# A hybrid decoder block on one Trainium2 core: due times for a plan's last weight splits, a sum of weights by an adding transfer, and the norm's ScalarE steps one tile at a time

## The chip, the cores and the metric

The kernel runs on one core of one Trainium2 chip. The metric is the device time of one execution in microseconds; lower is better. A trace of one profiled execution is at hand beside the times. Engines are named as the profile names them: PE multiplies matrices (PEld loads its weights), DVE is the vector engine, ACT the scalar engine, POOL the GpSimd engine, SP the engine that issues most transfers.

## The reference

One layer of a decoder trunk for 256 tokens and 16 learned meta tokens ahead of them, model width 2048, all in float32:

```python
u = RMSNorm(h)
z_pool, v_conv, g_conv, gate_a, gate_b = split(u @ w_in)      # 1024, 1024, 1024, 2048, 2048 columns
y_a = causal_multiscale_pool(z_pool, w_grp, scale) @ w_pool_out
a   = v_conv * sigmoid(g_conv)
c   = depthwise_conv(a, 31 taps) + b_dw
y_b = silu(layer_norm(c)) @ w_conv_out                        # the "conv matrix", 1024 x 2048
m   = sigmoid(gate_a) * y_a + sigmoid(gate_b) * y_b
h   = h + RMSNorm(m @ w_o)
h   = h + RMSNorm(relu(RMSNorm(h) @ w_up) ** 2 @ w_down)
return h[16:]                                                 # meta tokens dropped
```

## The kernel before

**Arithmetic.** Every float32 weight block of 128 x 2048 elements (1 MB) is split into a rounded part `hi` (a cast on ACT, L283, L1005) and the rest `lo` (a subtraction on DVE, L286, L1009). Each product is three matmuls: activation high by weight high, high by low, low by high. A block product for 128 tokens is 12 matmuls on PE. There are three places for a `hi` and three for a `lo`; the split of a block can only start once PE has used up the block three places before it.

**Stages.** In order of time: the projections of `w_in` (v, g, z, then eight column blocks of gates, `acc_gate`, L846, two accumulators for the two halves of the tokens, four weight blocks each); inside them, ahead of the last gate column block, the small products of the pooling groups (`pooled_groups`, `acc_grp`, L500); the conv matrix (L1086); the pooling matrix `w_pool_out` (`acc_po`, L846); `w_o`; then the MLP, more than half of the time. The change touches the end of the gates and the conv matrix.

**Order of the work in the gates.** Each engine works through its own queue in the order in which the program issues. `fetch()` (called once ahead of the products of each weight block) opens and splits the block two further on, and then issues the steps collected in `late`. After each half block (12 matmuls) `drain` gives 1.45 us of credit to a list `pending`, whose items carry a cost, and issues items from its front while the credit lasts. An item `FETCH` in the list holds it up until `late` is empty; `LATER` ends that drain. The layer norm behind the depthwise convolution is such a list: the statistics, `ln_newton`, then `normed` on two halves of four channel tiles (DVE, L816), then for each of the eight channel tiles two ACT steps (`affine`: a sigmoid, L821, and the scaled copy, L822), then `swish` (DVE, L827, two halves). In the kernel before, `normed` puts the affine steps of its half into `late`, so all eight pairs are issued in one go at the next `fetch()`, behind that block's split, and the two `swish` follow in the next two drains.

**Accumulators.** Six PSUM banks carry the tag of `acc_tile`, two that of `misc_tile`; banks are handed out in the order in which they came free. `pooled_groups` makes eight accumulators: six from the first kind and two from the second. The two accumulators of the gate column block that follows are therefore in the banks of group products 0 and 1. Each group product is read by an ACT step (L925) and a DVE step (L926), and those DVE steps stand in the queue behind the split of the block that `pooled_groups` fetches.

**The conv matrix.** Columns 0 to 1023 are done with a seven-product scheme for a 2 x 2 matrix of blocks (units "1" to "7"), the others plainly ("X20" and so on, each for two token halves "a" and "b"). `UNITS` is the order of the products on PE. Four blocks are loaded into `blocks_room` and summed there on DVE (L999): `SUM_C` says into which and from which. Units 1, 6, 7 and 4 accumulate in one bank, "ch"; behind 1, 6 and 7 its value is copied out on ACT (`keep`, L1036) before the next of them may add to it. `joined` and `gate_conv` (DVE, L1045, L1040) put the results together and multiply them by the gates. The last two entries of the stage (called "pool" in the code) are splits of the first two blocks of `w_pool_out`; their products come only after the stage.

**The planner.** The stage is written as a list of (engine, cost, reads, writes) and ordered by `Plan`. PE's items keep their order, and their costs added up give each a time; every other item gets a due time from the PE items that depend on it. The planner then plays the list through with the costs and always takes, on each engine, among the items that could start within 0.15 us of the earliest, the one with the earliest due time. An item on which no PE item of the plan depends has no due time and goes last. Before the change these are the two "pool" splits and most of the gate multiplications.

Of the kernel before, what the change touches and what calls it, by code (L numbers as in the profile page):

```python
# [11 lines left out]
AF = mybir.ActivationFunctionType  # L12
# [103 lines left out]
def hybrid_block(ctx: ExitStack, tc: tile.TileContext, ins: dict, out: bass.AP):  # L116
# [105 lines left out]

    UNITS = "X20a X20b X21a X21b X30a X30b 1 5 2 6 X31a X31b 7 3 4".split()
    CONV = list(dict.fromkeys(u_.rstrip("ab") for u_ in UNITS))
# [587 lines left out]
    def ln_items(q0):  # L812
        c = conv["c"][:, q0:q0 + QW, :]

        def normed():
            nc.vector.tensor_mul(c, c, wide(ln["r"]))  # L816

            def affine():
                for q in range(q0, q0 + QW):
                    g_b = dict(scale=col("conv_ln_g", q), bias=col("conv_ln_b", q))  # L820
                    nc.scalar.activation(ln["sq"][:, q, :], conv["c"][:, q, :], AF.Sigmoid, **g_b)  # L821
                    nc.scalar.activation(conv["c"][:, q, :], conv["c"][:, q, :], AF.Identity,  # L822
                                         **g_b)
            late.append(affine)

        def swish():
            nc.vector.tensor_mul(c, c, ln["sq"][:, q0:q0 + QW, :])  # L827

        def high():
            nc.scalar.copy(ln["out"][:, q0:q0 + QW, 0, :], c)  # L830

        def low():
            nc.vector.tensor_sub(ln["out"][:, q0:q0 + QW, 1, :], c,
                                 f32(ln["out"][:, q0:q0 + QW, 0, :]))
        return [(1.1, f) for f in (normed, swish, low, high)]

    ln_halves = ln_items(0), ln_items(QW)
    for step in range(2):
        pending += [FETCH] + [half[step] for half in ln_halves]

# [117 lines left out]
    BLOCK_C = ((0, 0), (0, 1), (1, 1), (1, 0))  # L958
    SUM_C = {"5": (0, 1), "6": (0, 2), "4": (0, 3), "7": (1, 2)}
    conv_banks = {"ch": misc_tile("acc_co_chain"), "w2": misc_tile("acc_co_2"),  # L960
# [23 lines left out]
    def load_block(i):  # L984
        cplan.add("SP", 3.1, lambda: nc.sync.dma_start(
            blocks_room[:, i].rearrange("p (k c) -> p k c", k=CK), conv_block(*BLOCK_C[i])[0]),
            writes=(f"block{i}",), late=3.0)

    def split_c(e, key):

# [20 lines left out]
        cplan.add("ACT", 1.83, high, reads=(name,), writes=(f"hi{q}",))  # L1011
        cplan.add("DVE", 2.22, low, reads=(name, f"hi{q}"), writes=(f"lo{q}",))

    def form_parts(key):
# [99 lines left out]
    while split_done < len(CONV) + 2:  # L1114
        split_c(split_done, "pool")
        split_done += 1
    assert not wanted_c
    cplan.emit()
    for e in ahead_p:
# [1168 lines left out]
```

## Time and profile before

| what | value |
|---|---|
| median of 3 runs | 1189.6 us (1188.96 to 1190.41) |
| profiled execution | 1189.37 us |
| its span in the trace | 1187.7 us |
| PE busy | 1173.8 us (99%) |
| DVE busy | 1034.4 us (87%) |
| ACT busy | 690.0 us (58%) |
| mean granted PE clock | 0.996 |

All times of day below are microseconds from the start of the trace's span. A row of the timeline gives start, duration, engine, line, operation, output<-inputs, shape and count; in brackets stands how long the engine had been idle before it and what released it. Neighbouring instructions of one kind are merged into a row with their count. A row of a table of windows gives the window, its length, the busy time with the number of instructions, the granted clock as a share of full speed, the busy share of the transfer engines and GB/s. A row of waits gives who waited for whom: total, times, longest.

### The profile page before, as it was taken

The numbers are of one execution on the slowest core, as the hardware profiler recorded it, in microseconds if no ns is written. First come the engines' busy times: TensorE is split into PE (matmuls) and PEld (weight loads), VectorE is DVE, ScalarE is ACT, GpSimd is POOL, SyncE is SP. The second block draws the span as 40 slices with busy tenths as digits, with TensorE's granted clock in tenths as the row PEclk, the third lists the DMA queues.
The fourth block names the chain that finished last, engine by engine and source line by source line (L and its number), as shares of the span: only waits on it lengthen the run. The fifth ranks groups of instructions, "written<-read, shape, count | busy, mean of one in ns | idle before, by whom it ended". The sixth has DMA issues, their size and how long they took to land.

```text
span 1187.7 us, 15784 instructions
## 1 busy us (share of the span) xinstructions
PE 1173.8 (99%) x6339; PEld 1018.4 (86%) x6339; DVE 1034.4 (87%) x1113; ACT 690.0 (58%) x701; POOL 45.0 (4%) x51
## 2 busy tenths in 40 slices
PE   9999999999999999999999999999999999999997
PEld 9999988888887788898888888888888888888886
DVE  6899989987689699987998988989989989889865
ACT  6543344446755466756565766666656666666642
POOL 1000000000000000000001001000000010010000
PEclk9999999999999999999999999999999999999998
DMA  8655555655573967849868999798998998998861
GB/s 294 213 178 178 186 202 181 203 186 177 202 259 130 288 211 221 283 145 335 238 211 248 240 282 249 219 292 215 301 274 213 276 279 229 280 244 240 304 212 72
DMA packets 177883, 272.91 MB, mean 230 GB/s; under 512 B 4658, under 2 KB 92914, under 8 KB 176913
## 3 DMA queue, kind: packets, MB, share of 16 engines
q1 hardware_dynamic: 160176, 235.88, 58.3%
q0 software_dynamic: 16736, 34.76, 16.1%
q10 hardware_dynamic: 896, 1.25, 0.3%
q8 instruction: 50, 0.82, 0.3%
q14 instruction: 25, 0.20, 0.0%
HBM read 267.68 MB, written 4.19 MB: 229 GB/s over the span
## 4 chain that ended last, share of the span: by engine, by line
PE 93%; DVE 3%; DMA 2%; ACT 1%; issue 1%; DVEq 0%; ACTq 0%
PE bank_u L505 18%; PE acc_gate L846 13%; PE bank_a L2002 10%; PE bank_u L511 9%; PE acc_up L2002 8%; PE bank_b L2002 7%; PE o_c L1385 6%; PE acc_z L500 4%; PE acc_v L500 3%; PE acc_g L500 3%; PE acc_vg L500 2%; DMA raw<-in_w_pool_out_dram 2%; PE acc_up L505 1%; DVE lo L286 1%; PE bank_u L2002 1%; PE acc_ca L1086 1%
## 5 line engine op out<-in xcount | busy, mean ns | idle before, releaser
L505 PE MATMUL bank_u<-m,hi 128*128 128x512 f32 x960 | 329.4, 390 | 0.0
L511 PE MATMUL bank_u<-m,lo 128*128 128x256 f32 x960 | 265.5, 277 | 0.0
L283 ACT CAST hi<-raw 128x2048 fp32r<-128x2048 f32 (+2 forms) x86 | 135.5, 1591 | 157.0 <-PE acc_gate L846 31.7
L505 PEld LDWEIGHTS bank_u<-m,hi 128*128 128x128 f32 x960 | 180.2, 188 | 37.8
L286 DVE TENSOR_TENSOR lo<-raw,hi 128x2048 fp32r<-128x2048 f32 (+2 forms) x86 | 161.6, 1891 | 38.3 <-ACT hi L283 38.1
L1785 DVE TENSOR_TENSOR lo<-raw_m,hi 128x2048 fp32r<-128x2048 f32 x70 | 160.1, 2288 | 31.9 <-ACT hi L1781 31.8
L511 PEld LDWEIGHTS bank_u<-m,lo 128*128 128x128 f32 x960 | 180.3, 188 | 1.4
L1781 ACT CAST hi<-raw_m 128x2048 fp32r<-128x2048 f32 x70 | 133.9, 1913 | 74.4 <-DVE raw_m L1798 21.3
L846 PE MATMUL acc_gate<-hi,u_um 128*128 128x512 f32 x416 | 131.0, 389 | 0.0
L566 DVE SCALAR_TENSOR_TENSOR c<-a,taps,c 128x256 f32<-128x256 f32 x240 | 98.6, 478 | 0.1
L2002 PE MATMUL bank_a<-hi,forms 128*128 128x512 f32 (+1 forms) x288 | 93.5, 386 | 0.0
L846 PEld LDWEIGHTS acc_gate<-hi,u_um 128*128 128x128 f32 x416 | 78.1, 188 | 16.2
L846 PE MATMUL acc_gate<-lo,u_um 128*128 128x512 f32 x208 | 80.9, 389 | 0.0
L1781 ACT CAST hi<-raw_a 128x2048 fp32r<-128x2048 f32 x29 | 55.4, 1910 | 35.1 <-PE bank_u L505 13.6
L1785 DVE TENSOR_TENSOR lo<-raw_a,hi 128x2048 fp32r<-128x2048 f32 x29 | 66.3, 2287 | 10.8 <-ACT hi L1781 10.7
L1781 ACT CAST hi<-raw_c 128x2048 fp32r<-128x2048 f32 x27 | 51.5, 1908 | 26.8 <-PE bank_u L505 12.4
L1785 DVE TENSOR_TENSOR lo<-raw_c,hi 128x2048 fp32r<-128x2048 f32 x27 | 61.7, 2286 | 5.2 <-ACT hi L1781 5.1
L2002 PEld LDWEIGHTS bank_a<-hi,forms 128*128 128x128 f32 x288 | 53.9, 188 | 11.0
L1785 DVE TENSOR_TENSOR fourth_pair<-raw_m,fourth_pair 128x2048 fp32r<-128x2048 f32 x26 | 59.4, 2286 | 4.3 <-ACT fourth_pair L1781 4.3
L1865 ACT COPY half<-bank_u 128x256 f32<-128x256 f32 x60 | 22.2, 370 | 66.0 <-PE bank_u L511 66.0
L2002 PE MATMUL acc_up<-hi,forms 128*128 128x512 f32 x176 | 57.5, 390 | 0.0
L2002 PE MATMUL bank_a<-lo,forms 128*128 128x512 f32 (+1 forms) x144 | 55.6, 386 | 0.0
(457 smaller groups left out, 2334.4 us busy)
## 6 DMA issues: line engine op xcount, KB each, us to landing
raw<-in_w_in_dram SPq DMA_DIRECT2D x52, 1024.0 KB, 5.0
raw_m<-in_w_down_dram SPq DMA_DIRECT2D x38, 1024.0 KB, 7.0
raw_m<-in_w_down_dram POOLq DMA_DIRECT2D x22, 1024.0 KB, 10.0
raw_a<-in_w_up_dram SPq DMA_DIRECT2D x20, 1024.0 KB, 6.5
raw_c<-in_w_up_dram SPq DMA_DIRECT2D x19, 1024.0 KB, 7.4
raw_m<-in_w_up_dram SPq DMA_DIRECT2D x19, 1024.0 KB, 7.1
raw_a<-in_w_down_dram SPq DMA_DIRECT2D x13, 1024.0 KB, 7.1
raw_c<-in_w_down_dram SPq DMA_DIRECT2D x13, 1024.0 KB, 7.1
```

What stands on the lines that cost most here:

```text
L283: nc.scalar.copy(hi[:, sl, cs], raw[:, sl, cs])
L286: nc.vector.tensor_sub(lo[:, sl, cs], raw[:, sl, cs], f32(hi[:, sl, cs]))
L500: nc.tensor.matmul(acc, w[:, k[0], cs], act[:, k[1], a, off:], start=first and n == 0, stop=last and n == 2)
L505: nc.tensor.matmul(acc.rearrange("p (a t) -> p a t", a=2)[:, :, ts], hi[:, k[0], cs], act[:, k[1], :, off + ts.start:off + ts.stop], start ...
L511: nc.tensor.matmul(acc[:, :T], lo[:, k[0], cs], act[:, k[1], 0, off:], start=False, stop=stop, skip_group_check=True)
L566: nc.vector.scalar_tensor_tensor(c, conv["a"][:, q, i:i + T], taps[:, q, i:i + 1], c, op0=ALU.mult, op1=ALU.add)
L846: nc.tensor.matmul(acc, act(kk)[:, a_, ts_], w_[:, k, :], start=kk == 0 and n == 0, stop=kk == nk - 1 and n == 2)
L1385: nc.tensor.matmul(acc, form(k, a_), box[w_][:, k, :], start=start and k == 0 and n == 0, stop=stop and k == CK - 1 and n == 2, skip_group ...
L1781: nc.scalar.copy(box["hi"], raw)
L1785: nc.vector.tensor_sub(box["lo"], raw, f32(box["hi"]))
L1865: nc.scalar.copy(box[j], accs[j][:, :T])
L2002: nc.tensor.matmul(acc, forms[h][:, f, k, a_, :], box[w_][:, k, cs], start=start and k == 0 and n == 0, stop=stop and k == KH - 1 and n == ...
```

## The change

Four things change.

1. In `UNITS` units 7 and 3 change places: "3 7 4" in place of "7 3 4".
2. The sum of weights for unit 7 is no longer a DVE addition of block 2 to block 1. A transfer issued by POOL reads block (1, 1) of the conv matrix from memory once more and adds it to block 1 in place, once the sum for unit 5 has read block 1.
3. For each of the two "pool" splits an empty PE item of 5.44 us is put at the end of the plan that reads its `hi` and `lo`. It issues nothing; it gives the splits a due time.
4. The affine steps leave `late`. They become eight items of the pending list, one for each channel tile, at a cost of 0.7; a `LATER` and the two `swish` follow.

```diff
--- before.py
+++ after.py
@@ -220,7 +220,7 @@
     def conv_block(kb, n):
         return columns(w_conv_out, kb * CK, CK, n * CW)[0]
 
-    UNITS = "X20a X20b X21a X21b X30a X30b 1 5 2 6 X31a X31b 7 3 4".split()
+    UNITS = "X20a X20b X21a X21b X30a X30b 1 5 2 6 X31a X31b 3 7 4".split()
     CONV = list(dict.fromkeys(u_.rstrip("ab") for u_ in UNITS))
     stream += [conv_block(int(key[2]), int(key[1])) for key in CONV[:2]]
     for n in range(NB):
@@ -815,14 +815,6 @@
         def normed():
             nc.vector.tensor_mul(c, c, wide(ln["r"]))
 
-            def affine():
-                for q in range(q0, q0 + QW):
-                    g_b = dict(scale=col("conv_ln_g", q), bias=col("conv_ln_b", q))
-                    nc.scalar.activation(ln["sq"][:, q, :], conv["c"][:, q, :], AF.Sigmoid, **g_b)
-                    nc.scalar.activation(conv["c"][:, q, :], conv["c"][:, q, :], AF.Identity,
-                                         **g_b)
-            late.append(affine)
-
         def swish():
             nc.vector.tensor_mul(c, c, ln["sq"][:, q0:q0 + QW, :])
 
@@ -835,8 +827,14 @@
         return [(1.1, f) for f in (normed, swish, low, high)]
 
     ln_halves = ln_items(0), ln_items(QW)
-    for step in range(2):
-        pending += [FETCH] + [half[step] for half in ln_halves]
+    def affine(q):
+        def f():
+            g_b = dict(scale=col("conv_ln_g", q), bias=col("conv_ln_b", q))
+            nc.scalar.activation(ln["sq"][:, q, :], conv["c"][:, q, :], AF.Sigmoid, **g_b)
+            nc.scalar.activation(conv["c"][:, q, :], conv["c"][:, q, :], AF.Identity, **g_b)
+        return f
+    pending += [FETCH] + [half[0] for half in ln_halves]
+    pending += [(0.7, affine(q)) for q in range(KC)] + [LATER] + [half[1] for half in ln_halves]
 
     def block_t(acc, hi, lo, act, kc, nk, t, ks=range(CK)):
         ts_ = slice(t * P, (t + 1) * P)
@@ -956,7 +954,7 @@
     blocks_room = big.tile([P, 4, CK * CW], F32, tag="um", name="conv_blocks")
     ROOM_C = {"1": 0, "5": 0, "6": 0, "4": 0, "7": 1, "3": 2, "2": 3}
     BLOCK_C = ((0, 0), (0, 1), (1, 1), (1, 0))
-    SUM_C = {"5": (0, 1), "6": (0, 2), "4": (0, 3), "7": (1, 2)}
+    SUM_C = {"5": (0, 1), "6": (0, 2), "4": (0, 3)}
     conv_banks = {"ch": misc_tile("acc_co_chain"), "w2": misc_tile("acc_co_2"),
                   "w3": acc_tile("acc_co_3")}
     BANK_C = {"1": "ch", "6": "ch", "7": "ch", "4": "ch", "2": "w2", "5": "w3", "3": "w3"}
@@ -986,6 +984,11 @@
             blocks_room[:, i].rearrange("p (k c) -> p k c", k=CK), conv_block(*BLOCK_C[i])[0]),
             writes=(f"block{i}",), late=3.0)
 
+    def add_block(to, i):
+        cplan.add("POOL", 5.6, lambda: nc.gpsimd.dma_start(
+            blocks_room[:, to].rearrange("p (k c) -> p k c", k=CK), conv_block(*BLOCK_C[i])[0],
+            accum_op=ALU.add), reads=(f"block{to}",), writes=(f"block{to}",), late=6.5)
+
     def split_c(e, key):
 
         q, n = slot_c(e), first_c + e
@@ -1010,6 +1013,8 @@
             conv_parts[e] = tuple(box[h].rearrange("p (k c) -> p k c", k=CK) for h in HALVES)
         cplan.add("ACT", 1.83, high, reads=(name,), writes=(f"hi{q}",))
         cplan.add("DVE", 2.22, low, reads=(name, f"hi{q}"), writes=(f"lo{q}",))
+        if key == "5":
+            add_block(1, 2)
 
     def form_parts(key):
 
@@ -1115,6 +1120,8 @@
         split_c(split_done, "pool")
         split_done += 1
     assert not wanted_c
+    for e in ahead_p:
+        cplan.add("PE", 5.44, lambda: None, reads=[f"hi{slot_c(e)}", f"lo{slot_c(e)}"])
     cplan.emit()
     for e in ahead_p:
         opened.append((*conv_parts[e], [], flats[e]))
```

## The prediction

> **What bounds the kernel now.** I read the page first, then PE's waits, then the granted clock, then the timelines of the two stages that the change touches.
>
> ```profile
> PE 1173.8 (99%) x6339; PEld 1018.4 (86%) x6339; DVE 1034.4 (87%) x1113; ACT 690.0 (58%) x701; POOL 45.0 (4%) x51
> ```
>
> PE is busy 99% of the span, so whatever is won or lost is won or lost in gaps of PE and in its clock. The waits of PE between 300 and 440 us name its gaps; outside there is only the start:
>
> ```profile
> PE acc_po L846 <- DVE lo L1009: 2.1, 1, 2.1
> PE acc_grp L500 <- DVE lo L286: 0.9, 1, 0.9
> PE mt L1140 <- ACT m L1144: 0.7, 1, 0.7
> PE mt L1140 <- DVE mts L1159: 0.3, 1, 0.3
> ...
> ```
>
> They lie between 306 and 423 us, and the change touches the engines' queues ahead of the first two. The first costs more than its 2.1 us:
>
> ```profile
> 305.00:309.00 4.00, 3.11 (x21) 1.00 0.14 14
> ...
> 376.00:380.00 4.00, 1.94 (x7) 0.88 0.39 79
> 380.00:384.00 4.00, 4.00 (x14) 0.70 1.02 417
> ```
>
> Behind the idle time at 376 the granted clock falls: a deficit of 0.12 x 4 + 0.30 x 4 = 1.68 us of full-speed work. Behind the 0.9 us at 306 it stays at 1.00. So a gap near 2 us in this kernel costs its length plus 1.7; one near 1 us only its length.
>
> **The norm's steps, tile by tile (first place, 294 to 314 us).**
>
> ```profile
> 294.15 0.60 ACT L821 ACTIVATE sq<-c,vecs 128x256 f32<-128x256 f32 x1 [2.14 <-DVE c L816]
> ...
> 303.19 3.70 ACT L283 CAST hi<-raw 128x2048 fp32r<-128x2048 f32 x2
> 306.80 1.25 ACT L877 ACTIVATE sg<-acc_gate,r_in 128x512 f32<-128x512 f32 x2
> ```
> ```profile
> 298.81 1.23 DVE L827 TENSOR_TENSOR c<-c,sq 128x1024 f32<-128x1024 f32 x1 [1.41 <-ACT c L822]
> 303.31 1.22 DVE L827 TENSOR_TENSOR c<-c,sq 128x1024 f32<-128x1024 f32 x1 [3.28 <-ACT c L822]
> 305.12 4.50 DVE L286 TENSOR_TENSOR lo<-raw,hi 128x2048 fp32r<-128x2048 f32 x2 [0.58 <-ACT hi L283]
> 309.87 2.29 DVE L286 TENSOR_TENSOR lo<-raw,hi 128x2048 fp32r<-128x2048 f32 x1 [0.26 <-ACT hi L283]
> 312.08 3.22 DVE L926 SCALAR_TENSOR_TENSOR y<-acc_grp,vecs,y 128x256 fp32r<-128x256 f32 x8
> ```
> ```profile
> 306.18 0.40 PE L500 MATMUL acc_grp<-d,hi 128*128 128x256 f32 x2
> 307.46 0.39 PE L500 MATMUL acc_grp<-d,lo 128*128 128x256 f32 x1 [0.89 <-DVE lo L286]
> ...
> 313.06 0.40 PE L846 MATMUL acc_gate<-hi,u_um 128*128 128x512 f32 x1
> ```
>
> Eight affine pairs take ACT from 294.15 to 303.19, 1.13 us each; two `hi` casts stand behind them, and PE at 306.18 lacks the `lo` of the pooling weights. Afterwards I follow the credit. `normed` leaves 0.35 (2.55 less 2 x 1.1). The two drains of the next block issue pairs 0-1 and 2-3, those of the block after it 4-5 and 6-7, and `LATER` ends there. The two `swish` come in the drains of the block that follows, the last before `pooled_groups`.
> ACT: pairs 0 to 3 to 298.7, `hi` of the pooling weights to 300.5, pairs 4 to 7 to 305.0, the next `hi` to 306.9. The same work, so from 306.80 ACT stands as before. DVE: `lo` of the pooling weights 300.6 to 302.9, in time for 306.18. The gap is gone, and PE ends the group products at 313.06 less (307.46 - 306.18 - 2 x 0.12), that is at 312.0.
> But the queue of DVE now reads `lo` (next gate block), `swish`, `swish`, `lo` (third row above), L926. Before, the `swish` ran in holes ahead of both `lo`. Now `lo` runs 306.9 to 309.1, the two `swish` (1.14 each in a row) to 311.4, the next `lo` to 313.6, the first L926 to 314.1. The gate products that follow write the bank of group product 0, which that L926 releases. Before, the bank was free at 312.56 (the last row's first step, 0.48 long), half a microsecond ahead of PE. Now PE arrives at 312.0 and starts at 314.15: a wait of 2.15 us takes the place of 0.9. Net: 314.15 - 313.06 = **+1.1 us**, before the clock. The ends for the wait are 0 (if `swish` runs elsewhere) and 2.15 + 1.7. I take 2.15 with the fall of the clock, since 2.06 us idle is the nearest row and brought it.
>
> The Trainium skill, "TensorE: Matmul & The Clock Gate", section "Why this matters for your kernels", wants no idle gaps above about 3 us and would let a gap of 2 us pass; by that rule the sum below would be 1.7 us lower. The fall behind 2.06 us idle in the windows above speaks against it.
>
> **The conv matrix: due times, the order, the adding transfer (second place, 335 to 392 us).**
>
> ```profile
> 344.80 4.62 DVE L999 TENSOR_TENSOR conv_blocks<-conv_blocks 128x2048 f32<-128x2048 f32 x2
> 349.33 2.28 DVE L1009 TENSOR_TENSOR lo<-conv_blocks,hi 128x2048 fp32r<-128x2048 f32 x1
> ...
> 365.42 0.68 DVE L911 TENSOR_TENSOR conv_forms<-c,conv_forms 128x512 fp32r<-128x512 f32 x1
> ...
> 369.68 2.29 DVE L1009 TENSOR_TENSOR lo<-conv_blocks,hi 128x2048 fp32r<-128x2048 f32 x1 [0.17 <-ACT hi L1005]
> 371.89 0.69 DVE L1040 TENSOR_TENSOR sg<-pairs,sg 128x512 f32<-128x512 f32 x1
> ...
> 376.21 2.28 DVE L1009 TENSOR_TENSOR lo<-raw_c,hi 128x2048 fp32r<-128x2048 f32 x1
> ```
> ```profile
> 354.09 0.59 ACT L1036 COPY pairs<-acc_co_chain 128x512 f32<-128x512 f32 x1 [0.77 <-PE acc_co_chain L1086]
> ...
> 362.25 1.91 ACT L1005 CAST hi<-conv_blocks 128x2048 fp32r<-128x2048 f32 x1 [0.67 <-PE acc_co_chain L1086]
> ...
> 370.41 1.92 ACT L1005 CAST hi<-raw_c 128x2048 fp32r<-128x2048 f32 x1 [0.77 <-PE acc_co_chain L1086]
> 372.61 0.59 ACT L1036 COPY pairs<-acc_co_chain 128x512 f32<-128x512 f32 x1 [0.28 <-DVE sg L1040]
> ```
> ```profile
> 367.49 0.39 PE L1086 MATMUL acc_co_chain<-hi,conv_forms 128*128 128x512 f32 x1
> ...
> 370.21 0.39 PE L1086 MATMUL acc_co<-hi,conv_forms 128*128 128x512 f32 x1
> ...
> 372.70 0.39 PE L1086 MATMUL acc_co<-hi,conv_forms 128*128 128x512 f32 x1
> 373.25 0.50 PE L1086 MATMUL acc_co_chain<-hi,s_act 128*128 128x512 f32 x1 [0.15 <-ACT pairs L1036]
> ...
> 376.10 0.39 PE L846 MATMUL acc_po<-hi,y 128*128 128x512 f32 x1
> 378.55 0.50 PE L846 MATMUL acc_po<-lo,y 128*128 128x512 f32 x1 [2.06 <-DVE lo L1009]
> ...
> 396.40 1.03 PE L1140 MATMUL mt<-ident,mts 128*128 128x128 f32 x8
> ```
>
> *Due times.* The `hi` of the first pool block is ready at 372.33, but its `lo` starts at 376.21, behind seven gate steps that have no due time either. With one it goes ahead of them: I played the planner's list through by hand, and DVE's order becomes `lo` of unit 4, one gate step, `lo` of the first pool block (372.5 to 374.8), two gate steps, `lo` of the second (375.9 to 378.2), then the rest. PE wants the first at 376.3 and the second 5.44 us later. The gap goes, and with it the fall of the clock. If a step of 0.6 us came ahead of the `lo` after all, it would still end at 375.4. The rest of the gate steps end near 381, the next `lo` behind them at 383.5, wanted at 387: hidden by PE's 10.9 us on two blocks.
>
> *The adding transfer* takes a 2.3 us sum off DVE. It is worth about nothing on PE: it ran in a hole, since the `lo` at 349.33 had to wait for a `hi` until then anyway. Two gate steps without due time move into the hole. The transfer may start at 347.1, behind the first of the two sums, and is wanted by the `hi` of unit 7 at 362.8, the place of the `hi` at 362.25 behind one step of 0.5:
>
> ```profile
> raw_m<-in_w_down_dram POOLq DMA_DIRECT2D x22, 1024.0 KB, 10.0
> ...
> DMA to landing us min/median/max: 5.8/11.7/19.2
> ```
>
> POOL's 22 transfers of this kind in the MLP land after 10.0 us (median), so at 357 to 358: hidden, with 5 us to spare. POOL has nothing queued behind it until `early_sums` at 377. Ends: 0, and the slowest landing of the four `early_sums` transfers, 19.2 us in the last row (a rival below).
>
> *3 7 4.* A unit takes 2.72 us (367.49 to 370.21). Unit 3 now wants its split and its form at 367.49; they take the places that unit 7's had in DVE's queue, and the form there ended at 366.10 (365.42 + 0.68), 1.4 us ahead. Units 7 and 4 add to one bank, and unit 7's value must be copied out between them. Before, unit 3 covered the copy; now PE waits for it. By the copy behind unit 1 (354.09, 0.59 long) and its hand-over to PE at 373.25: end of unit 7 at 372.93 (0.23 behind the last matmul's start), copy 372.97 to 373.56, unit 4 at 373.61, against 373.25 before: **+0.36 us**. ACT is free then, since the pool `hi` ends at 372.33.
>
> Together: the first pool product moves from 376.10 to 376.46, and from there to the transposes (396.40) 72 matmuls run without gap, at 2.72 / 12 = 0.227 each: 392.8 instead of 396.4. **-3.6 us.**
>
> **Behind it (392 to 423 us).**
>
> ```profile
> 402.76 1.91 ACT L283 CAST hi<-raw 128x2048 fp32r<-128x2048 f32 x1 [0.72 <-DMA raw<-in_w_pool_out_dram]
> ...
> 409.80 0.63 PE L1140 MATMUL mt<-ident,mts 128*128 128x128 f32 x4 [0.70 <-ACT m L1144]
> ```
>
> The wait of 0.70, and that of 0.3 in the waits above, come from a late landing: the `hi` at 402.76 waits for its block, and the sums that the transposes need stand behind its `lo`. That transfer is issued when a raw buffer comes free. The earlier pool splits free two buffers 3.7 us sooner, in a stretch where the transfer engines were nearly idle, so I expect the landing some microseconds sooner and both waits gone: **-1.0 us**. The other end: if it stays at 402.7, its `lo` at 407 is wanted by PE at 405.6, which gives back 1.4. From 423 us on PE has no named wait, so the shift is carried to the end.
>
> **Sum**, against the profiled execution of 1189.37 us: +1.1 + 1.7 (clock) - 3.6 - 1.0 = -1.8, that is 1187.6. The median, 1189.6, lies 0.2 above that execution, which is inside the spread; I leave it at **1187.6**.
>
> **Rivals.**
> (a) The new wait doesn't bring the clock down: 1187.6 - 1.7 = **1185.9**. For it: the trace has one gap of that length, so how often the clock falls behind it isn't known. Against it: it did fall there. Chance 0.19. The Trainium skill's rule named above would give this time.
> (b) The tile-by-tile steps take the wait at 306 away and no bank wait comes: 1189.4 - 1.1 - 3.6 - 1.0 = **1183.7**. Against it: `swish` stands behind `lo` in the queue by the credit. Chance 0.08.
> (c) The adding transfer lands late and stalls unit 7 and all splits behind it. With a landing after 19.2 us (366.5) `hi` 7 ends at 368.4, `hi` 4 at 370.9, unit 4's `lo` at 374.3, the gate step and the copy at 375.5: unit 4 starts at 375.6, 2.0 late, 1189.6. Each further microsecond costs one: it is slower than before from 19.2 us on, and at 22 us **1192.4**. For it: DVE is busy throughout. Against it: POOL's transfers of the MLP land in 10 us beside a busy DVE. Chance 0.08. The Trainium skill, "SBUF — State Buffer", section "SBUF: two separate sides", tells of DVE operations that keep POOL from writing a transfer's descriptors, which would give this time; the 10.0 us row shows no sign of it.
> (d) The due times don't help, since the splits are bound by their places and the gap stays: 1189.4 + 1.1 + 0.4 = **1190.9**, or 1192.6 with a second fall of the clock. For it: `hi` of the second pool block can only start when unit 7 is through. Against it: 372.33 to 376.21 is a plain wait in DVE's queue. Chance 0.10.
>
> **How the numbers follow.** The forecast has 0.55 (alone 1186.6 to 1190.0: the wait of 2.15 may be a microsecond shorter, the last term may turn to +1.4). A measurement here can tell about 0.2%, 2.4 us: faster is below 1187.2, slower above 1192.0. Faster: (a), (b) and a quarter of the forecast, 0.41. Slower: part of (c) and (d), 0.07. The range from 1185.0 to 1190.5 leaves out (b) and the far parts of (c) and (d).
>
> **What would show it.** Right: no idle time before L500 near 306, a wait of about 2 us on DVE L926 before `acc_gate` near 312 with the clock down behind it; no wait at the first `acc_po`; 0.5 to 0.7 us before unit 4, on ACT L1036; the transposes near 410 without wait. Wrong: `swish` (L827) ahead of the `lo` at 306.9, a PE wait before unit 7, or `acc_po` still waiting.

## The result, and the profile after

| | median of the runs | lowest to highest |
|---|---|---|
| before | 1190.26 us (14 runs) | 1188.41 to 1191.72 |
| after | 1188.48 us (14 runs) | 1186.88 to 1192.29 |

The ratio is 0.999 with a 95% interval of 0.998 to 1.0001: 1.8 us less in the medians, and the interval holds the ratio 1, so the runs don't tell it from no change. The profiled execution of after took 1188.6 us, its span 1186.9 us, against 1189.37 and 1187.7 of before.

The waits of PE in after, from 300 to 440 us (who waited for whom: total, times, longest):

```profile
PE acc_gate L844 <- DVE y L924: 2.0, 1, 2.0
PE mt L1147 <- DVE mts L1166: 1.3, 1, 1.3
PE mt L1147 <- ACT m L1151: 0.7, 1, 0.7
PE acc_co_chain L1091 <- ACT pairs L1041: 0.7, 1, 0.7
```

The two waits of before that the change aimed at (0.9 on `lo` L286, 2.1 on `lo` L1009) are gone. A wait of 2.0 at the gate products (L844, L846 of before) is new, the copy wait in the conv matrix is 0.7, and the waits at the transposes (L1147, L1140 of before) have grown and moved: 0.7 near 410 and 0.3 near 422 in before, 1.3 and 0.7 in after, both near 421. The windows of PE show which of these gaps touch the clock:

```profile
304.00:308.00 4.00, 4.00 (x26) 1.00 0.75 257
...
312.00:316.00 4.00, 1.96 (x6) 0.76 0.71 215
316.00:320.00 4.00, 4.00 (x16) 0.82 0.56 209
376.00:380.00 4.00, 3.57 (x16) 1.00 0.32 78
380.00:384.00 4.00, 4.00 (x19) 1.00 0.99 352
...
416.00:420.00 4.00, 3.38 (x15) 1.00 0.08 29
420.00:424.00 4.00, 2.65 (x15) 1.00 0.80 262
```

The fall of the clock stood between 376 and 384 us in before and stands between 312 and 320 us in after: a deficit of 0.24 x 4 + 0.18 x 4 = 1.68 us, as in before. Why PE waits at 312 stands in DVE's timeline of after:

```profile
306.83 2.29 DVE L286 TENSOR_TENSOR lo<-raw,hi 128x2048 fp32r<-128x2048 f32 x1 [4.03 <-ACT hi L283]
309.04 2.35 DVE L819 TENSOR_TENSOR c<-c,sq 128x1024 f32<-128x1024 f32 x2
311.31 2.29 DVE L286 TENSOR_TENSOR lo<-raw,hi 128x2048 fp32r<-128x2048 f32 x1
313.52 3.22 DVE L924 SCALAR_TENSOR_TENSOR y<-acc_grp,vecs,y 128x256 fp32r<-128x256 f32 x8
```

Both `swish` (L819) stand between the two gate `lo`, and the step that frees the bank (L924) starts at 313.52. PE's timeline of after, at the places where before had or has a wait:

```profile
306.33 0.28 PE L500 MATMUL acc_grp<-d,lo 128*128 128x256 f32 x1
...
314.05 0.79 PE L844 MATMUL acc_gate<-hi,u_um 128*128 128x512 f32 x1 [2.04 <-DVE y L924]
...
376.43 0.50 PE L1091 MATMUL acc_co_chain<-hi,s_act 128*128 128x512 f32 x1 [0.68 <-ACT pairs L1041]
...
379.53 0.39 PE L844 MATMUL acc_po<-lo,y 128*128 128x512 f32 x1
...
407.43 1.04 PE L1147 MATMUL mt<-ident,mts 128*128 128x128 f32 x8
...
420.66 0.63 PE L1147 MATMUL mt<-ident,mts 128*128 128x128 f32 x4 [1.28 <-DVE mts L1166]
421.98 0.63 PE L1147 MATMUL mt<-ident,mts 128*128 128x128 f32 x4 [0.70 <-ACT m L1151]
```

Set against the same matmul of before (after minus before in us; the places are times of before), the lead and the lag run like this:

| place | after - before |
|---|---|
| group products, 306 | -1.13 |
| first gate product behind them, 314 | +0.99 |
| after the fall of the clock, 320 | +2.7 |
| unit 4, 376 | +3.19 |
| first pool block, 384, where the clock of before is full again | -0.77 |
| transposes near 408 | -1.93 |
| transposes near 422 | -0.15 |
| MLP, 541 to 562 | from -0.16 to -0.74, little by little |
| last matmul | -0.74 |

From +2.7 at 320 to -1.93 at 408 are 4.6 us won; 2.7 of them only make good what the gates had lost, and of the 1.93 that are left the second transposes take back 1.78. The end of the chain that takes them back stands in ACT's timeline of after:

```profile
399.92 1.91 ACT L283 CAST hi<-raw 128x2048 fp32r<-128x2048 f32 x1
407.47 1.91 ACT L283 CAST hi<-raw 128x2048 fp32r<-128x2048 f32 x1 [5.64 <-DMA raw<-in_w_pool_out_dram]
```

and in that of before:

```profile
402.76 1.91 ACT L283 CAST hi<-raw 128x2048 fp32r<-128x2048 f32 x1 [0.72 <-DMA raw<-in_w_pool_out_dram]
407.25 1.91 ACT L283 CAST hi<-raw 128x2048 fp32r<-128x2048 f32 x1 [2.58 <-DMA raw<-in_w_pool_out_dram]
```

The sixth pool block comes 2.8 us sooner in after, the seventh, at 407.4, does not. All that the transposes near 421 need stands behind its `hi` in the queues. In after's timeline of DVE that is:

```profile
409.41 2.29 DVE L286 TENSOR_TENSOR lo<-raw,hi 128x2048 fp32r<-128x2048 f32 x1 [2.60 <-ACT hi L283]
411.62 0.68 DVE L1154 TENSOR_TENSOR m<-mt,m 128x512 fp32r<-128x512 f32 x1
...
416.90 2.29 DVE L286 TENSOR_TENSOR lo<-raw,hi 128x2048 fp32r<-128x2048 f32 x1
419.10 0.69 DVE L1165 TENSOR_TENSOR mts<-acc_po,sg 128x512 f32<-128x512 f32 x1
419.82 0.69 DVE L1166 TENSOR_TENSOR mts<-mts,sg 128x512 f32<-128x512 f32 x1
```

In the lines left out are the second `m` and the four sums into `A` (L1175 to L1178). From the `hi` at 407.47 to the end of `mts` at 420.51 this chain takes 13.0 us, and PE's transpose starts at 420.66. What held the landing was to be found out.

### The profile page after: what moved, and what is told of

The parts are those of the page before. It is cut to its first block, busy times and chain, and to the rows that moved or that the text cites. A ratio compares the mean times of both kernels' runs of the same rounds, so it can differ in the third digit from the quotient of the medians.

```text
span 1186.9 us, 15785 instructions
## 1 busy us (share of the span) xinstructions
PE 1172.6 (99%) x6339; PEld 1018.2 (86%) x6339; DVE 1031.9 (87%) x1112; ACT 689.3 (58%) x701; POOL 46.4 (4%) x52
## 4 chain that ended last, share of the span: by engine, by line
PE 94%; DVE 2%; ACT 2%; DMA 2%; issue 0%; DVEq 0%; ACTq 0%
PE bank_u L505 18%; PE acc_gate L844 13%; PE bank_a L2009 10%; PE bank_u L511 9%; PE acc_up L2009 8%; PE bank_b L2009 7%; PE o_c L1392 6%; PE acc_z L500 4%; PE acc_v L500 3%; PE acc_g L500 3%; PE acc_vg L500 2%; DMA raw<-in_w_pool_out_dram 2%; PE acc_up L505 1%; PE acc_co_chain L1091 1%; PE acc_po L844 1%; PE bank_u L2009 1%
## 5 line engine op out<-in xcount | busy, mean ns | idle before, releaser
L286 DVE TENSOR_TENSOR lo<-raw,hi 128x2048 fp32r<-128x2048 f32 (+2 forms) x86 | 161.6, 1889 | 43.4 <-ACT hi L283 43.3
L844 PE MATMUL acc_gate<-hi,u_um 128*128 128x512 f32 x416 | 132.4, 392 | 2.0 <-DVE y L924 2.0
L844 PEld LDWEIGHTS acc_gate<-hi,u_um 128*128 128x128 f32 x416 | 78.9, 190 | 18.6 <-DVE y L924 2.2
L844 PE MATMUL acc_gate<-lo,u_um 128*128 128x512 f32 x208 | 81.5, 392 | 0.0
```

Source lines behind the costliest of these rows:

```text
L286: nc.vector.tensor_sub(lo[:, sl, cs], raw[:, sl, cs], f32(hi[:, sl, cs]))
L844: nc.tensor.matmul(acc, act(kk)[:, a_, ts_], w_[:, k, :], start=kk == 0 and n == 0, stop=kk == nk - 1 and n == 2)
```

## The experiments

Medians, and the ratio to before with its 95% interval. Each group of runs has its own runs of before beside it, with medians from 1189.87 to 1190.26; gains below are against those.

| run | median us | ratio | waits of PE over 0.3 us, 300 to 440 us, and near what time |
|---|---|---|---|
| after | 1188.48 | 0.9990 [0.9980, 1.0001] | 2.04 at 312, 0.68 at 376, 1.28 + 0.70 at 421 |
| a1_no_affine | 1187.79 | 0.9972 [0.9962, 0.9981] | 0.89 at 306, 0.68 at 373, 2.08 at 418 |
| a2_affine_only | 1191.75 | 1.0014 [1.0005, 1.0023] | 2.04 at 312, 2.07 at 381, 0.93 + 0.70 at 412, 0.34 at 426 |
| a3_due_only | 1187.05 | 0.9971 [0.9960, 0.9982] | 0.88 at 306, 1.92 + 0.42 at 418 |
| a4_order_add_only | 1189.16 | 0.9991 [0.9982, 1.0000] | 0.89 at 306, 0.68 at 374, 0.34 at 377, 0.36 + 0.70 at 406, 1.63 + 0.70 at 421 |
| b1_swish_early | 1187.33 | 0.9976 [0.9967, 0.9985] | 0.52 at 312, 0.68 at 373, 1.55 + 0.70 at 418 |
| c1_one_swish | 1188.44 | 0.9982 [0.9972, 0.9991] | 0.91 at 312, 0.68 at 373, 2.05 + 0.70 at 419 |
| b2_no_early_adds | 1186.82 | 0.9965 [0.9951, 0.9979] | 2.04 at 312, 0.68 at 376 |
| d2_after_late_adds | 1187.30 | 0.9978 [0.9969, 0.9988] | 2.04 at 312, 0.68 at 376, 1.32 at 436 |
| b3_due_swish_early | 1187.22 | 0.9971 [0.9960, 0.9981] | 0.53 at 312, 1.50 + 0.70 at 417 |
| d3_due_swish_adds | 1183.28 | 0.9942 [0.9929, 0.9954] | 0.53 at 312 |
| d5_all_swish_adds | 1183.64 | 0.9947 [0.9933, 0.9960] | 0.52 at 312, 0.68 at 373 |
| e1_late_adds_only | 1187.45 | 0.9975 [0.9966, 0.9984] | 0.89 at 306, 2.06 at 378, 0.67 at 396, 0.36 at 420, 0.35 at 430 |

### Which part does what

The change without its fourth part (the affine steps stay in `late`):

```diff
-    pending += [FETCH] + [half[0] for half in ln_halves]
-    pending += [(0.7, affine(q)) for q in range(KC)] + [LATER] + [half[1] for half in ln_halves]
+    for step in range(2):
+        pending += [FETCH] + [half[step] for half in ln_halves]
```

> The changed kernel with the norm's ScalarE steps put back as they were before (issued in one go, swish ahead of the next splits); unit order 3 7 4, the adding transfer and the due times stay. Theory (the norm's steps cost, the due times gain): a PE wait of 0.9 us near 306 again, none of 2 us near 312 and no fall of the clock there; the first pool product at 376.5 without a wait; PE some 3.6 us ahead of the kernel before at the first transposes. Time 2.5 to 3.5 us below the kernel before. Rival (the norm's steps gain by themselves, the wait near 312 comes from something else): the wait near 312 stays and the time is not below that of the changed kernel.

The fourth part alone, on the kernel before (the same lines the other way round):

> The kernel before with nothing but the norm's ScalarE steps tile by tile. Theory: the wait of 0.9 us near 306 goes, a wait of about 2 us on the pooling groups' DVE steps comes near 312, PE leaves it 1.0 us later than before, and 2.7 us later where the clock falls; the wait of 2 us at the first pool product stays with its own fall of the clock. Time 1 to 3 us above the kernel before. Rival: faster than before by 1 us, the wait near 306 gone and nothing in its place.

The due times alone:

```diff
+    for e in ahead_p:
+        cplan.add("PE", 5.44, lambda: None, reads=[f"hi{slot_c(e)}", f"lo{slot_c(e)}"])
```

> The kernel before with nothing but the two empty PE items; order 7 3 4 and the DVE sum for unit 7 as before. Theory (the due times alone carry the gain, the adding transfer is worth nothing): no wait at the first pool product, which stays at 376.1, no fall of the clock; PE 3.9 us ahead of the kernel before at the first transposes, of which the transposes near 410 to 422 give back 0 to 2 where they wait for the seventh pool block's landing. Time 2.5 to 3.9 us below the kernel before. Rival (DVE must lose the 2.3 us sum as well): a wait of 1 us or more stays at the first or second pool block.

The order 3 7 4 and the adding transfer alone:

```diff
-    UNITS = "X20a X20b X21a X21b X30a X30b 1 5 2 6 X31a X31b 7 3 4".split()
+    UNITS = "X20a X20b X21a X21b X30a X30b 1 5 2 6 X31a X31b 3 7 4".split()
...
-    SUM_C = {"5": (0, 1), "6": (0, 2), "4": (0, 3), "7": (1, 2)}
+    SUM_C = {"5": (0, 1), "6": (0, 2), "4": (0, 3)}
... (add_block as in the change)
+        if key == "5":
+            add_block(1, 2)
```

> The kernel before with unit order 3 7 4 and the adding transfer alone; no due times, the norm's steps as before. Theory: the pool splits still stand behind the gate steps in DVE's queue, two of which have moved into the hole that the sum leaves, so the wait at the first pool product shrinks by about 1.2 us at most, to 0.9 to 2; 0.7 us of wait before unit 4. Time 0.5 us above to 2.5 us below the kernel before, the lower end where the clock no longer falls. Rival (the transfer carries the gain): 3 to 4 us below the kernel before, no wait at the first pool product.

The change without its fourth part is 2.3 us faster than before (1187.79 against 1190.13), a little less than the 2.5 to 3.5 that were expected: the gates and the conv matrix went as said, with PE 3.9 us ahead at the first transposes, but of the 4.8 us that it has behind them the transposes near 420 take 3.6 back, by a wait of 2.08 us and a fall of the clock behind it. The fourth part by itself makes the kernel 1.6 us slower (1191.75 against 1190.13) and brings the wait of 2.04; the due times by themselves make it 3.1 us faster, more than the whole change. The order and the adding transfer are worth 1.0 in the median. There I was wrong about the size of what is left at the pool products: 0.34 us on the `lo` and not 0.9 to 2, because unit 4 itself comes 0.6 later (its copy wait of 0.68), and the `lo` 1.1 sooner (PE starts on it at 377.42, at 378.55 before). Behind the 0.34 the clock stays at 1.00. The three parts add up to -2.4 us, the whole change gave -1.8.

In all three without the fourth part the waits at the transposes near 420 are longer than in before. With the due times alone PE is 5.3 us ahead of before at 404 and 1.9 at 424: 3.5 us given back where 0 to 2 were expected, since PE waits 2.3 us there and the clock falls behind it. The longest line of its waits:

```profile
PE mt L1142 <- DVE mts L1161: 2.3, 2, 1.9
```

and its windows there:

```profile
416.00:420.00 4.00, 1.69 (x9) 0.76 0.60 173
420.00:424.00 4.00, 4.00 (x17) 0.81 0.23 89
```

### The wait at 312: whose is it?

Each `swish` right behind its own four affine pairs, in the changed kernel:

```diff
-    pending += [(0.7, affine(q)) for q in range(KC)] + [LATER] + [half[1] for half in ln_halves]
+    pending += [(0.5, affine(q)) for q in range(QW)] + [(1.0, ln_halves[0][1][1])]
+    pending += [(0.5, affine(q)) for q in range(QW, KC)] + [(1.0, ln_halves[1][1][1])]
```

> The changed kernel with one thing moved: each of the two `swish` comes right behind its own four affine pairs, so DVE does both in the holes ahead of the two gate `lo`, as it did before the change. Theory (the wait of 2.0 us at `acc_gate` near 312 is the two `swish`, 1.14 us each, standing behind a `lo` in DVE's queue): the wait falls to 0 to 0.6 us, the granted clock stays at 1.00 from 312 to 320, the wait at 306 stays away. PE is then 2 us (wait) or 3.2 us (wait and clock) ahead of the changed kernel at 376 us. Of that the transposes near 420 us give back whatever the landing of the seventh pool block holds fast, as they gave back 1.8 us in the runs so far, so the time is 1 to 3 us under the changed kernel: 1185.5 to 1187.5 against 1188.5. Rival (the wait is owed to the splits of the pooling products alone, not to the `swish`): the wait stays at 2 us and the time is that of the changed kernel.

Only the first of them:

```diff
+    pending += [(0.5, affine(q)) for q in range(QW)] + [(1.0, ln_halves[0][1][1])]
+    pending += [(0.5, affine(q)) for q in range(QW, KC)] + [LATER, LATER, ln_halves[1][1]]
```

> The same move for the first `swish` alone; the second still stands behind the gate `lo`. Theory (each `swish` behind that `lo` is worth its 1.14 us): the wait at `acc_gate` near 312 is 0.9 to 1.1 us, half of the changed kernel's 2.0, and with so short a gap the granted clock stays at 1.00. Time: 1186.5 to 1188.5. If any wait there brings the clock down, whatever its length, 312 to 320 us shows a fall here too. Rival: the wait stays at 2.0.

The wait on L925 (L924 of after) is 2.04 with both `swish` behind the gate `lo`, 0.91 with one, 0.52 with none. The first step is one `swish` (2.04 - 0.91 = 1.13, against 1.14 for one); the second is less, since from then on the `lo` ahead of the step that frees the bank waits for its `hi` from ACT (0.66 us with both `swish` early) and no longer for a `swish`. The windows of PE with one `swish` behind the `lo`:

```profile
312.00:316.00 4.00, 3.27 (x14) 1.00 1.02 331
316.00:320.00 4.00, 4.00 (x19) 1.00 0.47 136
...
416.00:420.00 4.00, 1.25 (x9) 1.00 0.35 107
420.00:424.00 4.00, 4.00 (x21) 1.00 0.40 155
```

The clock stays at 1.00 behind 0.91 us. It also stays at 1.00 behind 2.05 and 0.70 us at 419, to which the section on the hardware comes back. With both `swish` early PE reaches the transposes near 404 with a lead of 5.3 us on before; by 425 it has 1.7, behind waits of 1.55 and 0.70 us and a fall of the clock. The medians are 1187.33 for both and 1188.44 for one, against 1188.48 of after; against the runs of before beside each, the gains are 2.5, 1.4 and 1.8 us. So the move of both is worth 0.8 to 1.2 us, at or under the lower end of what was expected (1 to 3), and that of one nothing that shows, though its wait is half.

### What holds the seventh pool block?

In after the transfer engines are full from 380 to 408, and they move less than they can: 356 GB/s and then 267. Its windows, in which the last two numbers are the busy share of the transfer engines and GB/s:

```profile
380.00:394.00 14.00, 14.00 (x63) 1.00 1.03 356
394.00:408.00 14.00, 14.00 (x70) 1.00 1.09 267
```

In that time run the two adding transfers of `early_sums`. The changed kernel without them:

```diff
-    for keys, op in ((((0, 0), (0, 1)), {}), (((0, 1), (1, 1)), {"accum_op": ALU.add})):
+    for keys, op in ((((0, 0), (0, 1)), {}),):
```

> The changed kernel without the two adding transfers into `early_sums`: two sums of weight blocks of w_o lack their second halves, so that part of the output projection is computed from other weights. 2 MB less to move between 386 and 408 us. Theory (the transposes near 420 us wait because the seventh pool block lands at 407.4, and it lands there because the adding transfers take its share): its `hi` starts several us sooner, at 399 to 404, the transposes near 420 don't wait (1.28 and 0.70 in the changed kernel), and the time is 1.5 to 2.5 us under the changed kernel. The wait of 2.0 at `acc_gate` and the clock behind it stay. Rival (the landing is bound by the raw buffer that comes free at 396 us and by the transfer's own time): the `hi` stays within a microsecond of 407 and so do the waits.

Its windows and then its `hi` of the seventh block on ACT:

```profile
380.00:394.00 14.00, 14.00 (x63) 1.00 1.04 395
394.00:408.00 14.00, 14.00 (x70) 1.00 0.51 168
```

```profile
402.22 1.91 ACT L283 CAST hi<-raw 128x2048 fp32r<-128x2048 f32 x1 [0.40 <-ACT hi L283]
```

402.22 against 407.47, with no wait for a transfer, and no wait at either transposes. The load of this block is issued at 389.2 us in both kernels; it lands 18.2 us later in after, and at most 8.0 us later here. The loads of pool blocks issued from 380 to 445 us take 7.8 us to land (median; 13.6 in after):

```profile
raw<-in_w_pool_out_dram SPq DMA_DIRECT2D x4, 1024.0 KB, 7.8
```

The median is 1.7 below after's (1.3 by the gains against the runs of before beside each), at the lower end of what was expected or under it. So it is the adding transfers that hold the seventh block. Then the complete kernel, with these transfers later:

```diff
-    for keys, op in ((((0, 0), (0, 1)), {}), (((0, 1), (1, 1)), {"accum_op": ALU.add})):
+    def early(keys, **op):
         for e, key in enumerate(keys):
             nc.gpsimd.dma_start(early_sums[:, e].rearrange("p (k c) -> p k c", k=CK),
                                 source_o(key), **op)
+    early(((0, 0), (0, 1)))
+    gate_add = const.tile([P, 1], F32, name="gate_add")
...
         project_t(y_of, KP, evac_merged(n), f"po{n}")
+        if n == 1:
+            nc.gpsimd.tensor_copy(gate_add, mts[:, NT * 2 - 1, :1])
+            early(((0, 1), (1, 1)), accum_op=ALU.add)
```

> The changed kernel, complete, with the two adding transfers into `early_sums` issued later: POOL first reads a value that the evacuation of the second pool output block writes, near 404 us, and only then issues them; they are wanted near 445 us. Theory as for the run without them: the `hi` of the seventh pool block starts at 399 to 404, no wait at the transposes near 420, time 1.5 to 2.5 us under the changed kernel, 1186 to 1187. The adding transfers then land by 425 us, and share the engines with the first loads of w_o, wanted from 431 us on. Rival: the loads of w_o behind it come late instead, with a new wait of PE between 423 and 450 us, and the time stays.

Both theory and rival came true. The waits at the transposes are gone, and another has come:

```profile
PE acc_gate L844 <- DVE y L924: 2.0, 1, 2.0
PE o_a L1397 <- DVE m L1156: 1.3, 1, 1.3
PE acc_co_chain L1091 <- ACT pairs L1041: 0.7, 1, 0.7
```

The transfers are now issued at 409 us and share the engines with the first load of `raw_o` (issued at 417), whose `hi` starts at 428.52 only, behind 5.66 us of waiting; the `m` that PE needs stands behind its `lo` and the next one. The median is 1187.30, 1.2 below after (0.8 by the gains), less than the 1.5 to 2.5 that were expected.

### All gaps at once

The due times and `swish` early, on the kernel before:

> The kernel before, with the due times of the two pool splits and the affine pairs tile by tile, each `swish` right behind its own pairs; the order 7 3 4 and the sum of weights on VectorE as before. Theory (the gaps are independent, and the transposes near 420 hold back whatever arrives there early): no wait at 306, 0 to 0.6 us near 312, none at the first pool product, PE some 4 to 5 us ahead of the kernel before at 405 us, and 2 to 3 of that given back at the transposes near 420, with or without a fall of the clock. Time 1186 to 1187.5, no better than the due times alone. Rival (the gains add up): 1185 or less.

The same with the adding transfers behind a value that exists near 396 us in place of the one at 407:

```diff
+            nc.gpsimd.tensor_copy(gate_add, A[:, NT - 1, 0, 0, :1])
```

> The run before this one, and the two adding transfers into `early_sums` issued later: POOL first reads a value of the transposed merged block (`A`, written near 396 us) and then issues them, near 399 us. When they were issued at 409 us they shared the engines with the load of `raw_o` issued at 417, and PE waited 1.3 us for it at 436; ten microseconds sooner they should be through by then. Theory (the seventh pool block's landing is the anchor): its `hi` starts near 399, no wait at the transposes near 420 and none over 0.5 us near 436; the 4 to 5 us stay: 1184 to 1185.5. Rival (every stretch is pinned by its next load, so a lead is always given back): some other wait of 1 to 3 us comes between 405 and 450 us, and the time stays at 1186 to 1187.5.

The changed kernel with both:

> The changed kernel with each `swish` right behind its own affine pairs (as in the run that did this alone) and the two adding transfers into `early_sums` issued behind the same value, near 399 us. Theory: 0.5 us near 312 and 0.7 us before unit 4 stay, the transposes near 420 don't wait (1.5 and 0.7 with `swish` early alone, and a fall of the clock behind them), no wait over 0.5 us near 436. Time 1184 to 1185.5, beside 1187.3 for `swish` early alone. Rival: as for the run before this one.

The late transfers alone, on the kernel before:

> The kernel before, with nothing but the two adding transfers into `early_sums` issued behind the read of `A`, near 399 us. Theory (the seventh pool block's landing is the anchor, and the kernel before arrives there late enough to lose only little by it): the waits of 0.7 and 0.3 us at the transposes near 410 and 422 go, the waits of 0.9 at 306 and 2.06 at 378 with the clock behind it stay, time 0.7 to 1.3 us under before. The two runs with all gaps closed and this move are 3.7 to 3.9 us under those without it; so the move would be worth 1 us alone and 3 to 4 us once the gaps ahead are closed. Rival (the move is worth its 3 to 4 us by itself): 1186 to 1187.

Closing the two gaps without moving the transfers gives 1187.22, no better than the due times alone, as expected: 1.50 and 0.70 us are waited at the transposes. With the transfers issued at 397 us the waits of the first of the two complete kernels are these two, all there are from 300 to 600 us:

```profile
PE acc_gate L845 <- DVE y L925: 0.5, 1, 0.5
PE acc_co_chain L1085 <- ACT pairs L1035: 0.2, 1, 0.2
```

and it takes 1183.28 us, 6.8 less than before (ratio 0.9942, interval 0.9929 to 0.9954); that is below the 1184 to 1185.5 that were expected. Its lead on before is 5.2 us at 405, 5.8 at 417 and 5.7 at the end: nothing is given back. With the order 3 7 4 and the adding sum as well it is 1183.64, 0.4 above it and also below what was expected; the runs of the two overlap: these two bring nothing once the due times are there.

The late transfers alone brought 2.7 us, neither the 1 of the theory nor the 3 to 4 of the rival. Its profiled execution doesn't explain them by waits: those at 306 and 378 are as before, those at the transposes came to 1.4 in place of 1.0. What its trace does show is that the clock did not fall behind the gap at 378:

```profile
376.00:380.00 4.00, 1.94 (x9) 1.00 0.46 113
380.00:384.00 4.00, 4.00 (x19) 1.00 1.02 395
```

That is 1.7 us in this one execution; why it did not fall stands in the section on the hardware. But this execution is only 1.1 us faster than the profiled one of before (1188.23 against 1189.37), and no other was traced, so where the 2.7 us of the medians come from stays open. All the same, closing the gaps (-2.8) and moving the transfers (-2.7) give -6.8 together, 1.3 more than the sum.

## Why the prediction was right or wrong

The forecast of 1187.6 lies 0.9 below the median of after and 1.0 below its profiled execution; the range held the time, and a change too small to be told was the likeliest outcome. Some of that is luck: a term of -1.0 came out as +0.6, a stretch that the prediction did not look at gave 0.6 back, and the median lies between the executions with a fall of the clock and those without. By its steps:

- **The norm's steps.** Right: the gap at 306 went, both `swish` moved behind the gate `lo`, and PE waits 2.04 us on the bank (2.15 said). The net is +0.99 (+1.1 said). The run with one `swish` and the run with none show that this is the cause.
- **The clock behind it, +1.7.** Right in the profiled execution (1.68). It isn't so in each execution: by the mean clocks five to seven of the fourteen had no fall, as in rival (a), to which I gave 0.19; but these took 1186.9 to 1188.4 us where rival (a) has 1185.9. I had it as one thing or the other. "A gap near 2 us costs its length plus 1.7" was read off one gap and is too simple: how the gap lies decides too (see the section on the hardware).
- **Due times.** Right: no wait at the first pool products, no fall there. From +2.7 behind the gates to -0.77 at 384 us is -3.4, with -3.6 said (the copy before unit 4 is part of both). Rival (d) is out.
- **The adding transfer.** Right: hidden, 9.8 us from issue to landing (10.0 said), no wait before unit 7. Rival (c) is out. (Its price was added up with a slip: 347.1 and 19.2 make 366.3 and not 366.5, so its times come out 0.2 lower.) After's row of transfers:

```profile
conv_blocks<-in_w_conv_out_dram POOLq DMA_DIRECT2D x1, 1024.0 KB, 9.8
```

- **3 7 4.** Right: 0.68 before unit 4 in place of 0.15, +0.53 (+0.36 said).
- **Behind it, -1.0.** Here the prediction failed. The first transposes went as said, -1.2 from 384 to 408 us. But at the next transposes, where before waited 0.34, after waits 1.28 and 0.70: +1.8 there, +0.6 for the term in place of -1.0. The step that failed is "I expect the landing some microseconds sooner". I read the landing off the `hi` at 402.76, the sixth block; that one did come sooner. The row below it, the `hi` at 407.25 with 2.58 us of waiting for its transfer, I had not looked at. It is the seventh block that the second transposes stand behind, and its transfer competes with two adding transfers that start with the same stage. I took the transfer engines for idle because they were so before the earlier splits; behind them they are full until 408. The end that I gave for this term, +1.4, was for the sixth block staying late, which is not what happened.
- **Not foreseen**: -0.6 between 541 and 562 us, little by little, where no wait is named in either trace. Its cause is open.

So at the last matmul the sum was -0.74 where -1.8 was said: 1.6 us less gain in the stretch behind and 0.2 less in the conv matrix, against 0.6 more in the MLP, 0.1 more at the bank, and 0.1 that after was ahead before the group products.

## What to carry to other kernels

A gap that is closed gives PE a lead, and the lead lives only until the next thing whose time does not depend on PE; here that was a transfer held by other transfers. So follow the lead to the next row that waits for a landing, read every such row up to the point where the queues are slack again, and ask what shares the engines with that transfer. When an operation is moved in an in-order queue, look at what comes to stand behind it: the wait of 2 us that came with the affine steps was two `swish` that had run in a hole before. And an experiment on one gap may show little until the next one is moved too: -2.8 and -2.7 alone, -6.8 together. When one trace shows a fall of the clock behind a gap, look at a second trace before the fall goes into a sum.

## What the runs showed of the hardware

**The clock behind gaps of 2 us.** Ten times in the fourteen profiled executions PE waited 1.92 to 2.08 us in one piece between 300 and 440 us. Behind eight of them the clock fell, at a cost of 1.7 us (deficits of 1.68 to 1.72 in the windows of 4 us); behind two it did not (2.06 at 378 with the transfers moved alone, 2.05 at 419 with one `swish` early). The gap at 378 is the same in before and in the run with the transfers moved alone, 2.06 us on the same `lo`, and fell in one and not in the other: the length of the gap doesn't settle it alone.

What settles it nearly always is how the gap lies. A trace records when the granted clock changes. In each of the fourteen the first entry is full clock, between 4.1 and 7.3 us of the span, and every later change lies a whole number of 3.413 us behind that entry. In before it is at 6.96 us, and the fall starts at 379.01, which is 109 of these steps later; in after the fall starts 90 steps behind the first entry, with the due times alone 121. A fall between 300 and 440 us goes to half the clock and lasts one step. So the time can be cut into stretches of 3.413 us from the first entry on. Around the gap at 378, two stretches of before:

```profile
375.60:379.01 3.41, 1.35 (x6) 1.00 0.27 22
379.01:382.43 3.42, 3.42 (x10) 0.50 0.91 369
```

and two of the run with the transfers moved alone:

```profile
373.83:377.25 3.42, 2.38 (x11) 1.00 0.00 0
377.25:380.66 3.41, 2.40 (x10) 1.00 0.74 214
```

In before the whole gap lies in one stretch, and the next has half the clock. In the other run an edge at 377.25 cuts it into 1.04 and 1.01 us, and the clock stays full. All places between 300 and 440 us where one wait, or two close together, come to more than 1.1 us:

| run | waits of PE, us | idle time in a stretch, us | clock in the next |
|---|---|---|---|
| b1_swish_early, 418 | 1.55 + 0.70 | 2.25 | half |
| a1_no_affine, 418 | 2.08 | 2.08 | half |
| a2_affine_only, 381 | 2.07 | 2.07 | half |
| before, 378 | 2.06 | 2.06 | half |
| a2_affine_only, after and d2_after_late_adds, 312 | 2.04 | 2.04 | half |
| b2_no_early_adds, 312 | 2.04 | 1.94 | half |
| c1_one_swish, 419 | 2.05 + 0.70 | 1.94, then 0.80 | full |
| a3_due_only, 418 | 1.92 | 1.92 | half |
| b3_due_swish_early, 417 | 1.50 + 0.70 | 0.43, then 1.77 | full |
| a2_affine_only, 412 | 0.93 + 0.70 | 1.58 | full |
| after, 421 | 1.28 + 0.70 | 0.48, then 1.49 | full |
| d2_after_late_adds, 436 | 1.32 | 1.32 | full |
| a4_order_add_only, 421 | 1.63 + 0.70 | 1.26, then 1.08 | full |
| e1_late_adds_only, 378 | 2.06 | 1.04, then 1.01 | full |

Nine stretches with 1.92 us of idle time or more were followed by half the clock, one with 1.94 was not, and none with 1.77 or less was. Two gaps close to each other add up when they lie in one stretch. By these runs the line is near 1.9 us; the one exception, and PE's ends, which are modelled, leave it open by some hundredths.

The first entry lies at another place in each trace, so one and the same gap can bring a fall in one execution and none in another. A fall weighs 1.7 of 1187 us, 0.0014 in the mean clock. The traced executions without a fall have mean clocks of 0.997 to 0.999, those with one 0.996 or 0.997, the one with two 0.995. After's 14 executions have 0.995 (three, 1191.88 to 1192.29 us), 0.996 (four, 1188.6 to 1190.15), and 0.997 and 0.998 (seven, 1186.88 to 1188.37): it fits that they differ by the number of such falls. That was read off the mean clocks only, which also count the low clock behind the last matmul, and the executions of before don't sort so: in the largest group those at 0.996 took 1189.04 to 1190.49 us and those at 0.997 1189.31 to 1191.86. The two kernels without a gap over 0.7 us stay within 0.9 us (1182.81 to 1183.70 and 1183.46 to 1184.18), but so nearly does the one with the transfers moved alone (1187.10 to 1188.23), gap of 2.06 and all.

The Trainium skill, "TensorE: Matmul & The Clock Gate", section "Why this matters for your kernels", would let all gaps under about 3 us pass; the eight falls behind 1.92 to 2.08 us say otherwise.

**Adding transfers slow the others down.** Two windows of after, the first with the two plain transfers into `early_sums` under way beside the loads, the second with the two adding ones:

```profile
382.00:386.00 4.00, 4.00 (x19) 1.00 0.94 363
394.00:398.00 4.00, 4.00 (x23) 1.00 1.10 259
```

With the adding transfers the engines are as busy as they get and move 258 to 265 GB/s (394 to 406 us); in the run that leaves these out they reach a busy share of 1.05 at 409 GB/s (390 to 394 us). A load of a pool block took 13.6 us to land (median) in place of 7.8. No run put plain transfers in their place, so that it is the adding, and not the 2 MB more, rests on these windows.

**POOL's read waits for DVE.** The copy of one value per partition that holds the late transfers back took 2.18 us in the run that read the merged block at 407 us, and 0.18 to 0.19 in the three that read `A` at 397 or 401. In the first, POOL's and DVE's timelines show that it ended with the `lo` that had started 0.15 us before it (407.03 + 2.18 = 409.21, 406.88 + 2.28 = 409.16):

```profile
407.03 2.18 POOL L1189 COPY gate_add<-mts 128x1 f32<-128x1 f32 x1 [25.31 <-DVE mts L1168]
```

```profile
406.88 2.28 DVE L286 TENSOR_TENSOR lo<-raw,hi 128x2048 fp32r<-128x2048 f32 x1
```

In the other three DVE had nothing to do at that time. The Trainium skill, "SBUF — State Buffer", section "Who interferes with whom", says that a DVE instruction with two inputs in SBUF contends with a POOL instruction that reads SBUF; this row agrees. It cost the late transfers 2 us there.
